# A two-layer hybrid diffusion trunk: weights loaded earlier at the start, PSUM operands in short VectorE chains, S5 states in fewer operations

## The chip, the cores and the metric

The kernel runs on one core of a Trainium2 chip. The metric is the time of one execution on the device in microseconds (us); the median of three runs stands for a kernel. One execution is also recorded by the profiler, and all rows below come from that one.

## What is computed

Two layers of one trunk, on a latent stream `x` of 512 tokens and a context of 256 tokens, both 1024 wide, in float32. The conditions `c` and `c_ctx` give six modulation vectors each (shift, scale and gate, twice). In each layer both streams go through four mixers side by side, are merged with gates, and pass a SwiGLU feed-forward part:

```python
mod_l = silu(c) @ w_ada[l] + b_ada[l]            # six vectors: sh1, sc1, g1, sh2, sc2, g2
h = rms_norm(x, norm1_g[l]) * (1 + sc1) + sh1    # the context the same way, with its own six
p = h @ w_in[l]                                  # columns for the four mixers and the gates
# S5: diagonal complex state space, forwards and backwards; gMLP; Mamba-2 SSD; latent attention
x = x + g1 * (merged @ w_out[l])
x = x + g2 * swiglu(rms_norm(x, norm2_g[l]) * (1 + sc2) + sh2)
```

`rms_norm` divides by the root of the mean square of a token's 1024 values. Latent attention norms its low-rank queries and keys once per token and then once per head; the SSD mixer norms its output, and gMLP has a layer norm. The context is not needed behind layer 1's mixers, so layer 1 carries it only as far as it is read.

## The kernel before, in words

Activations lie with channels on the 128 partitions and tokens along the free axis: eight tiles of 128 channels by 768 tokens, the first 256 the context (`CTXS`), the others the latent stream (`LAT`). Every large product is taken with each operand split into a high part in float32r and a low part that is the rest (`mm3`): three matmuls in place of one. Weights come in blocks of 1024 x 256 through two buffers (`weights`), ScalarE casts the high part, and GpSimd or VectorE subtracts the low part (`split`, L169 and L174).

The order on each engine is made by the framework's scheduler, which works through the program's instructions in program order with priorities, and holds an instruction back while its buffers are not free. The S5 mixer and the latent-attention pairs are generators that the program steps in turn, so that their small work lies between the projections.

What the change touches:

- **The start** (`run`, `ada_first`, `mix`). The latent stream is loaded, then `w_ada` for the first two vectors in three groups of columns (`ada_first`, L405), then the context and the first weights of `w_in`. The modulation is computed from the groups (`ada_chunk`), the latent stream normed (`norm_scale`) and modulated (`norm_mod`), then the context is transposed, normed and modulated. Only behind both stands `mix`, which takes the first two tiles of weights and projects them for the latent columns and then for the context's.
- **The norms** (`norm_scale`, `tok_rsqrt`, `rsqrt`). ScalarE squares eight tiles, VectorE adds them up in an SBUF tile (L174), a matmul with ones sums over channels, and `rsqrt` finds the inverse root per token: a bit estimate and two refinements, nine VectorE steps on 1 to 12 columns that each wait for the one before. `bcast_tok` puts the result on diagonals (L190), and a matmul spreads it. `mla_pair` uses `rsqrt` a second time, for six heads and two blocks of tokens.
- **The S5 mixer** (`s5_prep`, `s5_sixth`), in six parts a layer. `s5_prep` makes the operands of a sixth; four copies of 64x64 on VectorE (L479) stack real and imaginary halves. `s5_sixth` runs the scans and forms the states that enter each position, `sin`, in two tiles: forward and backward directions, real and imaginary halves, the backward ones written in reversed order, with three VectorE operations for each of four combinations.

Tiles from one pool carry its name: `sc`, `ty`, `f`, `g` and `h` are SBUF, `acc` (2 banks), `b1` (4) and `b5` (2) are PSUM and show as `acc` and `b`.

Of the kernel before, what the change touches and what calls it, by code (L numbers as in the profile page):

```python
# [12 lines left out]
I32 = mybir.dt.int32  # L13
AF = mybir.ActivationFunctionType
ALU = mybir.AluOpType
# [4 lines left out]
P = 128  # L20
D = 1024
KD = D // P
# [4 lines left out]
BR = 384  # L27
# [13 lines left out]
C_CQ = 2188  # L41
# [44 lines left out]
class Net:  # L86
# [116 lines left out]

    def rsqrt(s, y, x):
        t, u = s.ty(list(x.shape)), s.ty(list(x.shape))
        s.ts(y.bitcast(I32), x.bitcast(I32), -0.5, float(0x5F3759DF), ALU.mult, ALU.add)
        s.mul(t, y, y)
        s.mul(t, t, x)
        s.ts(u, t, 0.375, -1.25, ALU.mult, ALU.add)
        s.mul(u, u, t)  # L210
        s.stt(y, u, 1.875, y, ALU.add, ALU.mult)
        s.stt(t, y, -0.5, y, ALU.mult, ALU.mult)
        s.mul(t, t, x)
        s.stt(y, t, 1.5, y, ALU.add, ALU.mult)

# [53 lines left out]
    def tok_rsqrt(s, sq, nb, mul, eps):  # L269

        ps = s.b1()
        for b in range(nb):
            s.mm(ps[:, b * P:(b + 1) * P], sq[:, b * P:(b + 1) * P], s.ones)
        x, r = s.ty([P, nb]), s.ty([P, nb])
        s.ts(x, ps[:, 0:nb * P:P], mul, eps, ALU.mult, ALU.add)
        s.rsqrt(r, x)
        return r
# [118 lines left out]

    def ada_first(s, l):

        src = s.t["w_ada"][l].rearrange("(k p) f -> p k f", p=P)
        out = []  # L400
        for pool, tag, c, w, cuts in ((s.hp, "h", 0, 768, (0, 512, 768)), (s.hp, "h", 768, 768, (0, 256, 768)), (s.fp, "f", 1536, 512, (0, 512))):
            rows = []
            for k in range(KD):
                raw = pool.tile([P, w], F32, tag=tag, name=s.nm(tag))
                s.dma.dma_start(out=raw, in_=src[:, k, c:c + w])  # L405
                rows.append(raw)
            for a, b in zip(cuts, cuts[1:]):
                out.append(((c + a) // 256, b - a, [x[:, a:b] for x in rows]))
        return out

# [73 lines left out]
    def norm_scale(s, xs, off, n):  # L484

        sl = slice(off, off + n)
        a = s.sc()
        for k in range(KD):
            if k == 0:
                s.act(a[:, :n], xs[k][:, sl], AF.Square)  # L490
            else:
                q = s.sc()
                s.act(q[:, :n], xs[k][:, sl], AF.Square)
                s.add(a[:, :n], a[:, :n], q[:, :n])
        return s.bcast_tok(s.tok_rsqrt(a, n // P, 1.0 / D, 1e-6), n // P)
# [149 lines left out]
    def mla_pair(s, part, q, kd, off, t0, b0, xd, nk, nw, wh, wl, qk):  # L645

        eps = 1e-6
        w = 96 if part == "q" else 64
        hw = nw // 2
        x = s.st([P, nk, 256])  # L650
# [3 lines left out]
        sq, z = s.sc(), s.sc()  # L654
# [5 lines left out]
        r = s.tok_rsqrt(sq, 2, 1.0 / (nk * P), eps)  # L660
# [5 lines left out]
        for b in range(2):  # L666
            full = s.g()
            x = full[:, :576].rearrange("p (h d) -> p h d", d=96)
            z = s.st([P, 6, 96])
            for j in range(2):  # L670
                ps = s.b1()
# [13 lines left out]
        y, rs, rr = s.ty([P, 2, 6]), s.ty([P, 2, 6]), s.ty([P, 2, 6])  # L685
# [7 lines left out]
        s.ts(y, ms, 1.0 / 96, eps, ALU.mult, ALU.add)  # L693
        s.rsqrt(rs, y)
        s.mul(rr, rs, r.unsqueeze(2).to_broadcast([P, 2, 6]))
        gt, gc = q["rot"][part], q["gain"][:, 2 * (part == "kv") + (off == CTX):][:, :1]
        e = s.nc.gpsimd
        for b in range(2):
            x, full = tiles[b]
# [12 lines left out]
            y = full[:96].rearrange("p (h t) -> p h t", t=P)  # L712
            ps = [s.b1([P, 3, P]) for _ in range(2)]
# [368 lines left out]
    def s5_prep(s, l, i6):  # L1082

        gp, V = s.nc.gpsimd, s.nc.vector
        C, U = 96, 4
# [9 lines left out]
        for d in range(2):  # L1095
            o = 24 * l + 12 * d + 2 * i6
# [3 lines left out]
        x = [f_([P, U, C]) for _ in range(4)]  # L1100
# [13 lines left out]
        bbr, bbi, t1, t2 = (s.ty5([P, U, 16]) for _ in range(4))  # L1114
# [7 lines left out]
        for e in range(2):  # L1122
            s.vcopy(bbs[e][0:64], bbr[64 * e:64 * e + 64])
            s.vcopy(bbs[e][64:P], bbi[64 * e:64 * e + 64])

        pw = lambda k: G[:, k, :, 0:8].unsqueeze(3).to_broadcast([P, U, 8, 16])
        ch = lambda v: v.unsqueeze(2).to_broadcast([P, U, 8, 16])
        x = [f_([P, U, P]) for _ in range(4)]
# [37 lines left out]
    def s5_sixth(s, l, i6, ud, yd, segs):  # L1166
# [53 lines left out]
        yield  # L1220
        sin = [s.f([P, U, C]) for _ in range(2)]
        for e in range(2):
            gp.memset(sin[e][:, 0:2, 0:1], 0.0)
            gp.memset(sin[e][:, 2:4, 31:32], 0.0)
            r = slice(64 * e, 64 * e + 64)
            for w, (a, b, op) in zip((slice(0, 64), slice(64, P)), ((y[0], y[2], ALU.subtract), (y[1], y[3], ALU.add))):
                s.tt(sin[e][w, 0:2, 1:96], a[r, 0:2, 0:95], b[r, 0:2, 0:95], op)
                s.tt(sin[e][w, 2:4, 30::-1], a[r, 2:4, 0:31], b[r, 2:4, 0:31], op)
                s.tt(sin[e][w, 2:4, 95:31:-1], a[r, 2:4, 31:95], b[r, 2:4, 31:95], op)
        yield  # L1230
        ps = s.b5([C, 4, P])
        for i in range(2):
            for e in range(2):
                o = ps[:, 2 * i + e, :]
                s.mm(o, xf[:, 2 * i + e, :], tp[:, i, e, :], stop=False)
                s.mm(o, sin[e][:, i, :], ca[e][:, i, :], start=False, stop=False)
                s.mm(o, sin[e][:, 2 + i, :], ca[e][:, 2 + i, :], start=False)
        ys = s.f([C, 8, 4, 16])
# [41 lines left out]

    def mix(s, l, q, xs, xd, hh, hl, segs, rest, ws):

# [13 lines left out]
        def to_dram(d, segs_, f=None):  # L1296
            y = s.gs()

            def cb(ps, off, n, v):
                (f or s.act)(y[:, off:off + n], ps)  # L1300
                if off == segs_[-1][0]:
                    s.spill(d[:, off:], y[:, off:])
            return cb
# [11 lines left out]
        ws = ws or s.weights(w_in, C_CQ, BR)  # L1315
        pair = [(next(ws), to_dram(dq[c * P:(c + 1) * P], segs)) for c in range(2)]
        for sg in segs:
            for w, cb in pair:
                s.proj(w, hh, hl, [sg], cb)
        s.proj(next(ws), hh, hl, segs, to_dram(dq[2 * P:BR], segs))  # L1320
        next(load, None)
# [136 lines left out]

    def layer(s, l, q, f, xs, hh, hl, xd, extra, rest, late, then, ws=None):
        full = l < DEPTH - 1  # L1460
        segs = [LAT, CTXS] if full else [LAT]
        yd, gd = s.mix(l, q, xs, xd, hh, hl, segs, rest, ws)
        mh, ml = s.merge(l, yd, gd, segs)
# [71 lines left out]
    def run(s):  # L1535
# [3 lines left out]
        xr = s.load_x()  # L1539
        chunks = s.ada_first(0)  # L1540
        xr = s.load_ctx() + xr
        ws = s.weights(s.t["w_in"][0], C_CQ, BR)
        first = next(ws)
        q = turn({})
# [14 lines left out]
        def rest(a, lo, hi):  # L1559
            for i in range(lo, hi):  # L1560
                s.ada_chunk(a, i)
                yield
# [14 lines left out]
        next(norm)  # L1577
        next(xt)
        next(norm)
        s.params_more(0, q)  # L1580
        L8 = 21
        s.s5_scalars()
        ex = prepare()
# [9 lines left out]

        s.layer(0, q, a["f"], xs, hh, hl, xd, ex, rest(a, 8, L8), rest(a, L8, 24), then, chain([first], ws))
        xd = [s.dram(f"x1_{k}", [P, TOK]) for k in range(KD)]
# [34 lines left out]
```

## Time and profile before

| | before |
|---|---|
| median of three runs | 2789.63 us (2784.95 to 2795.59) |
| the profiled execution | 2790.0 us, span 2787.9 us |
| TensorE matmuls (PE) | 2626.4 us, 94% of the span |
| VectorE (DVE) | 1476.7 us, 53% |
| GpSimd (POOL) | 1211.5 us, 43% |
| ScalarE (ACT) | 940.7 us, 34% |
| mean granted TensorE clock | 0.978 |
| DMA | 397.32 MB, mean 143 GB/s |

A line of instructions reads: line of the program, engine, operation, output <- inputs by the program's names with their numbers left out, and shapes as partitions x elements. PE is TensorE's matmuls. A timeline row begins with the start and the length in us; xN means N instructions merged, and the bracket holds the idle time of the engine just before, with the instruction that ended it. Where several are merged, the length runs from the start of the first to the end of the last.

### The profile page before, as it was taken

What the parts mean: (1) busy time and instruction counts of PE and PEld (TensorE: products, weight loads), DVE (VectorE), ACT (ScalarE), POOL (GpSimd) and SP (SyncE); (2) the same over time, 40 slices, a digit from 0 to 9 for tenths busy, and PEclk for the clock granted to TensorE, in tenths of its full rate; (3) what the DMA queues carried; (4) which work ended last, traced back from release to release, by engine and by line L of the source; (5) the groups of instructions that cost most, each with busy time, mean ns of one, the idle gap of its engine ahead of it and who ended that gap; (6) DMA issues with size and microseconds to landing.
All of it is one profiled execution on the core that took longest, in us unless ns stands there. A gap on an engine that the chain in (4) does not pass through costs nothing. (4 is left out here: it accounts for less than half of the span.)

```text
span 2787.9 us, 39957 instructions
## 1 busy us (share of the span) xinstructions
PE 2626.4 (94%) x14964; PEld 2135.9 (77%) x14964; DVE 1476.7 (53%) x3088; ACT 940.7 (34%) x1805; POOL 1211.5 (43%) x901
## 2 busy tenths in 40 slices
PE   7998899999999998999999999999999999899999
PEld 4787777777888876888888877877766777678887
DVE  6667878647553768643321245676747446422111
ACT  4243344552222343222222234345552223322222
POOL 3254544324442836554433335443324536444443
PEclk8999999999999998999999999999999999999999
DMA  6655635445544645323322324566545546333332
GB/s 250 177 175 185 182 121 183 148 146 155 159 140 155 209 142 157 117 92 89 99 77 62 91 93 154 187 188 186 157 138 164 180 152 204 114 94 106 93 105 77
DMA packets 426040, 397.32 MB, mean 143 GB/s; under 512 B 53092, under 2 KB 372248, under 8 KB 425752
## 3 DMA queue, kind: packets, MB, share of 16 engines
q1 hardware_dynamic: 425848, 394.78, 45.8%
q8 instruction: 118, 1.93, 0.3%
q14 instruction: 74, 0.61, 0.1%
HBM read 305.66 MB, written 89.05 MB: 142 GB/s over the span
## 5 line engine op out<-in xcount | busy, mean ns | idle before, releaser
L174 POOL TENSOR_TENSOR wlo<-raw,whi 128x1024 fp32r<-128x1024 f32 (+2 forms) x314 | 629.2, 2005 | 1054.8 <-ACT whi L169 942.9
L193 PE MATMUL acc<-h,whi 128*128 128x512 f32 (+2 forms) x3424 | 1023.4, 369 | 20.0 <-DVE gs L186 7.6
L193 PE MATMUL acc<-h,wlo 128*128 128x512 f32 (+1 forms) x2024 | 747.8, 370 | 10.3 <-DVE wlo L174 5.5
L193 PEld LDWEIGHTS acc<-h,whi 128*128 128x128 f32 (+1 forms) x3424 | 613.4, 191 | 135.6 <-issue 15.7
L169 ACT CAST whi<-raw 128x1024 fp32r<-128x1024 f32 (+2 forms) x390 | 324.8, 834 | 775.3 <-PE b L193 300.8
L193 PEld LDWEIGHTS acc<-h,wlo 128*128 128x128 f32 x2024 | 385.2, 190 | 81.4 <-POOL wlo L174 8.5
L193 PE MATMUL acc<-g,whi 128*128 128x512 f32 (+1 forms) x840 | 270.2, 394 | 21.2 <-DVE g L174 8.1
L193 PE MATMUL acc<-f,whi 128*128 128x512 f32 (+1 forms) x600 | 230.4, 394 | 5.1 <-POOL f L174 5.1
L193 PE MATMUL b<-g,whi 128*128 128x256 f32 (+1 forms) x840 | 212.5, 331 | 3.3 <-ACT whi L169 3.3
L193 PE MATMUL b<-h,wlo 128*128 128x256 f32 (+1 forms) x624 | 203.6, 326 | 0.8 <-POOL wlo L174 0.8
L193 PE MATMUL b<-h,whi 128*128 128x256 f32 (+1 forms) x624 | 203.7, 326 | 0.0
L193 PEld LDWEIGHTS acc<-g,whi 128*128 128x128 f32 x840 | 153.2, 192 | 56.6 <-DVE g L174 11.7
L193 PE MATMUL b<-f,whi 128*128 128x256 f32 (+1 forms) x600 | 186.6, 321 | 1.5 <-ACT whi L169 1.5
L193 PE MATMUL b<-g,g 128*64 128x128 f32 (+5 forms) x915 | 177.8, 349 | 1.7 <-DVE g L190 1.1
L193 PEld LDWEIGHTS b<-g,whi 128*128 128x128 f32 x840 | 146.9, 191 | 28.1 <-ACT whi L169 6.5
L193 PE MATMUL acc<-g,wlo 128*128 128x512 f32 (+1 forms) x372 | 147.0, 395 | 4.3 <-DVE wlo L174 4.1
L186 DVE SCALAR_TENSOR_TENSOR sc<-sc,acc 128x512 f32<-128x512 f32 (+1 forms) x45 | 30.7, 681 | 218.9 <-ACT sc L171 218.9
L174 POOL TENSOR_TENSOR f<-f,f 128x384 f32<-128x384 f32 (+2 forms) x84 | 107.3, 1283 | 75.4 <-DVE f L174 36.5
L193 PEld LDWEIGHTS b<-g,g 128*128 128x128 f32 (+2 forms) x915 | 120.6, 180 | 22.7 <-issue 13.1
L174 POOL TENSOR_TENSOR g<-sc,g 128x256 fp32r<-128x256 f32 (+2 forms) x81 | 86.6, 1071 | 114.4 <-ACT g L169 88.3
L193 PEld LDWEIGHTS acc<-f,whi 128*128 128x128 f32 x600 | 113.0, 189 | 29.4 <-POOL f L174 6.6
L174 POOL TENSOR_TENSOR g<-g,sc 128x512 f32<-128x512 f32 (+1 forms) x82 | 102.6, 1261 | 68.5 <-DVE sc L186 35.7
(267 smaller groups left out, 3973.4 us busy)
## 6 DMA issues: line engine op xcount, KB each, us to landing
raw<-in_w_in_dram SPq DMA_DIRECT2D x50, 1024.0 KB
raw<-in_w_ffn_in_dram SPq DMA_DIRECT2D x88, 512.0 KB
raw<-in_w_ada_dram SPq DMA_DIRECT2D x40, 1024.0 KB
raw<-in_w_ffn_out_dram SPq DMA_DIRECT2D x36, 512.0 KB
gate<-gs SPq DMA_DIRECT2D x32, 384.0 KB
f<-s5w SPq DMA_DIRECT2D x48, 256.0 KB
raw<-in_w_branch_dram SPq DMA_DIRECT2D x32, 384.0 KB
gs<-gate SPq DMA_DIRECT2D x32, 384.0 KB
```

Source lines behind the costliest of these rows:

```text
L169: s.nc.scalar.copy(out=out, in_=x)
L174: (e or s.nc.vector).tensor_tensor(out=out, in0=a, in1=b, op=op)
L186: s.nc.vector.scalar_tensor_tensor(out=out, in0=a, scalar=sc, in1=b, op0=op0, op1=op1)
L193: s.nc.tensor.matmul(out=out, lhsT=l, rhs=r, start=start, stop=stop)
```

## The change

- `ada_first` takes a callback that it calls ahead of the third group of columns; `run` passes the loading and splitting of the first tile of weights, so this load of 1 MB (L525) is issued there and no longer behind the context.
- The context's transposes, norm and modulation, with the smaller parameters, go into a function `ctx` that `mix` calls behind the first tile's projection of the latent columns. `s5_scalars` moves behind the first two tiles.
- `rsqrt` computes the same two refinements in nine steps, ordered so that with `work` given each step has one operand in PSUM. `tok_rsqrt` passes two strips of the bank that it has, `mla_pair` a bank of its own. gMLP's five calls have no `work`. `norm_scale` adds up in a PSUM bank; the last addition writes SBUF.
- In `s5_prep` the four copies go to ScalarE. In `s5_sixth` VectorE writes `sin` for all four columns in forward order, four operations for twelve, and ScalarE writes the backward half reversed into a further tile `back`, in four copies.

```diff
-    def rsqrt(s, y, x):
-        t, u = s.ty(list(x.shape)), s.ty(list(x.shape))
-        s.ts(y.bitcast(I32), x.bitcast(I32), -0.5, float(0x5F3759DF), ALU.mult, ALU.add)
-        s.mul(t, y, y)
-        s.mul(t, t, x)
+    def rsqrt(s, y, x, work=None):
+
+        z, t = s.ty(list(x.shape)), s.ty(list(x.shape))
+        v, u = work or (y, s.ty(list(x.shape)))
+        s.ts(v.bitcast(I32), x.bitcast(I32), -0.5, float(0x5F3759DF), ALU.mult, ALU.add)
+        s.mul(z, x, v)
+        s.mul(t, z, v)
         s.ts(u, t, 0.375, -1.25, ALU.mult, ALU.add)
-        s.mul(u, u, t)
-        s.stt(y, u, 1.875, y, ALU.add, ALU.mult)
-        s.stt(t, y, -0.5, y, ALU.mult, ALU.mult)
-        s.mul(t, t, x)
-        s.stt(y, t, 1.5, y, ALU.add, ALU.mult)
+        s.mul(t, t, u)
+        s.stt(v, t, 1.875, v, ALU.add, ALU.mult)
+        s.mul(z, x, v)
+        s.stt(t, z, -0.5, v, ALU.mult, ALU.mult)
+        s.stt(y, t, 1.5, v, ALU.add, ALU.mult)
...
-        s.rsqrt(r, x)
+        s.rsqrt(r, x, [ps[:, c:c + nb] for c in (32, 40)])
...
-    def ada_first(s, l):
+    def ada_first(s, l, between):
...
             rows = []
+            if tag == "f":
+                done = between()
...
     def norm_scale(s, xs, off, n):
 
         sl = slice(off, off + n)
-        a = s.sc()
+        a, ps = s.sc(), s.b1()
         for k in range(KD):
             if k == 0:
-                s.act(a[:, :n], xs[k][:, sl], AF.Square)
+                s.act(ps[:, :n], xs[k][:, sl], AF.Square)
             else:
                 q = s.sc()
                 s.act(q[:, :n], xs[k][:, sl], AF.Square)
-                s.add(a[:, :n], a[:, :n], q[:, :n])
+                s.add((a if k == KD - 1 else ps)[:, :n], ps[:, :n], q[:, :n])
...
-        s.rsqrt(rs, y)
+        work = s.b1([P, 2, 2, 6])
+        s.rsqrt(rs, y, [work[:, j] for j in range(2)])
...
-            s.vcopy(bbs[e][0:64], bbr[64 * e:64 * e + 64])
-            s.vcopy(bbs[e][64:P], bbi[64 * e:64 * e + 64])
+            s.act(bbs[e][0:64], bbr[64 * e:64 * e + 64])
+            s.act(bbs[e][64:P], bbi[64 * e:64 * e + 64])
...
         sin = [s.f([P, U, C]) for _ in range(2)]
+        back = s.f([P, 2, 2, C])
         for e in range(2):
-            gp.memset(sin[e][:, 0:2, 0:1], 0.0)
-            gp.memset(sin[e][:, 2:4, 31:32], 0.0)
+            gp.memset(sin[e][:, :, 0:1], 0.0)
             r = slice(64 * e, 64 * e + 64)
             for w, (a, b, op) in zip((slice(0, 64), slice(64, P)), ((y[0], y[2], ALU.subtract), (y[1], y[3], ALU.add))):
-                s.tt(sin[e][w, 0:2, 1:96], a[r, 0:2, 0:95], b[r, 0:2, 0:95], op)
-                s.tt(sin[e][w, 2:4, 30::-1], a[r, 2:4, 0:31], b[r, 2:4, 0:31], op)
-                s.tt(sin[e][w, 2:4, 95:31:-1], a[r, 2:4, 31:95], b[r, 2:4, 31:95], op)
+                s.tt(sin[e][w, :, 1:96], a[r, :, 0:95], b[r, :, 0:95], op)
+
+            s.act(back[:, e, :, 31::-1], sin[e][:, 2:4, 0:32])
+            s.act(back[:, e, :, 95:31:-1], sin[e][:, 2:4, 32:96])
...
-                s.mm(o, sin[e][:, 2 + i, :], ca[e][:, 2 + i, :], start=False)
+                s.mm(o, back[:, e, i, :], ca[e][:, 2 + i, :], start=False)
...
-        pair = [(next(ws), to_dram(dq[c * P:(c + 1) * P], segs)) for c in range(2)]
-        for sg in segs:
+        pair = []
+        for c in range(2):
+            pair.append((next(ws), to_dram(dq[c * P:(c + 1) * P], segs)))
+            s.proj(pair[c][0], hh, hl, segs[:1], pair[c][1])
+            if c == 0 and ctx:
+                ctx()
+        for sg in segs[1:]:
             for w, cb in pair:
                 s.proj(w, hh, hl, [sg], cb)
+        if l == 0:
+            s.s5_scalars()
...
-        chunks = s.ada_first(0)
+        ws = s.weights(s.t["w_in"][0], C_CQ, BR)
+        chunks, first = s.ada_first(0, lambda: next(ws))
         xr = s.load_ctx() + xr
-        ws = s.weights(s.t["w_in"][0], C_CQ, BR)
-        first = next(ws)
...
-        next(xt)
-        next(norm)
-        s.params_more(0, q)
+
+        def ctx():
+            next(xt)
+            next(norm)
+            s.params_more(0, q)
```

The matmuls of the program are the same in kind and number. Three places show what moved.

First, GpSimd at the start. `wlo<-raw,whi` are the two splits of the first weights, `h<-sc,h` the low parts of the modulated latent stream, tile by tile. Before:

```order
L174 TENSOR_TENSOR h_449<-sc_457,h_441 128x512
L1004 MEMSET g_782 128x576
L1033 MEMSET g_834 128x48x4
L174 TENSOR_TENSOR h_451<-sc_465,h_443 128x512
...
L174 TENSOR_TENSOR h_455<-sc_481,h_447 128x512
L1057 MEMSET g_881 128x576
L174 TENSOR_TENSOR wlo_198<-raw_195,whi_197 128x1024
L174 TENSOR_TENSOR wlo_1082<-raw_195,whi_1081 128x1024
L174 TENSOR_TENSOR h_456<-sc_485,h_448 128x512
```

With the change:

```order
L174 TENSOR_TENSOR wlo_174<-raw_171,whi_173 128x1024
L1004 MEMSET f_937 128x48
L174 TENSOR_TENSOR wlo_731<-raw_171,whi_730 128x1024
L174 TENSOR_TENSOR h_450<-sc_458,h_442 128x512
L1009 MEMSET g_942 128x576
L1038 MEMSET g_994 128x48x4
L174 TENSOR_TENSOR h_452<-sc_466,h_444 128x512
```

The splits stood between the fifth and the sixth of GpSimd's subtractions and now stand ahead of the first.

Second, TensorE at the same place. `b<-k,f` transposes a block of the context, `acc<-h,whi` and `acc<-h,wlo` are the first projections of the latent columns. Before, the last of sixteen transposes and what follows:

```order
L197 MATMUL b_513<-k,f_193 128x128
L197 MATMUL b_517<-k,f_189 128x128
L197 MATMUL b_517<-k,f_193 128x128
L193 MATMUL acc_1086<-h_449,whi_197 128x512
L193 MATMUL acc_1086<-h_441,whi_197 128x512
```

With the change:

```order
L197 MATMUL b_571<-k,f_193 128x128
L193 MATMUL acc_537<-h_450,whi_173 128x512
L193 MATMUL acc_537<-h_442,whi_173 128x512
L193 MATMUL acc_537<-h_442,wlo_174 128x512
...
L193 MATMUL acc_735<-h_443,wlo_731 128x512
L197 MATMUL b_563<-k,f_197 128x128
```

Three of the context's transposes stand ahead of the first projections, the others between them.

Third, VectorE in the second norm of layer 0, context part: the last addition of the squares, the chain of `rsqrt` (`ty`, 128x2), and S5 products of layer 1's `s5_prep` (`h<-sx,sx`). Before:

```order
L174 TENSOR_TENSOR sc_10969<-sc_10969,sc_10989 128x256
L174 TENSOR_TENSOR h_11484<-h_11484,h_11485 128x512
L190 TENSOR_SCALAR ty_10995<-b_10992 128x2
...
L186 SCALAR_TENSOR_TENSOR ty_10998<-ty_10996 128x2
L174 TENSOR_TENSOR h_11633<-sx_11323,sx_11321 128x512
L174 TENSOR_TENSOR h_11635<-sx_11323,sx_11321 128x512
L174 TENSOR_TENSOR ty_10998<-ty_10998,ty_10995 128x2
L186 SCALAR_TENSOR_TENSOR ty_10996<-ty_10998,ty_10996 128x2
L190 TENSOR_SCALAR sc_11009<-k,ty_10996 128x128 x2
```

With the change:

```order
L174 TENSOR_TENSOR sc_10951<-b_10952,sc_10972 128x256
L174 TENSOR_TENSOR h_11467<-h_11467,h_11468 128x512
L190 TENSOR_SCALAR ty_10978<-b_10975 128x2
...
L174 TENSOR_TENSOR ty_10981<-ty_10978,b_10975 128x2
L174 TENSOR_TENSOR h_11616<-sx_11306,sx_11304 128x512
L174 TENSOR_TENSOR h_11618<-sx_11306,sx_11304 128x512
L186 SCALAR_TENSOR_TENSOR ty_10982<-ty_10981,b_10975 128x2
L186 SCALAR_TENSOR_TENSOR ty_10979<-ty_10982,b_10975 128x2
L190 TENSOR_SCALAR sc_10992<-k,ty_10979 128x128 x2
```

The neighbours are the same, two S5 products still stand inside the chain, and the chain's steps have a PSUM operand (`b`).

## Rows read from the trace of the kernel before

**Rows 1.** The page, part 1: busy time by engine, share of the span, instructions.
```profile
PE 2626.4 (94%) x14964; PEld 2135.9 (77%) x14964; DVE 1476.7 (53%) x3088; ACT 940.7 (34%) x1805; POOL 1211.5 (43%) x901
```
**Rows 2.** Waits of PE: waiter, what ended the wait; us in total, times, longest.
```profile
PE b L193 <- DVE sc L174: 14.2, 7, 4.0
...
PE b L193 <- DVE sc L190: 10.8, 3, 4.9
```
**Rows 3.** Timeline of PE at three places: start us, us, instruction, idle before.
```profile
247.59 1.49 PE L197 MATMUL b<-k,g 128*96 128x128 f32 x6 [9.92 <-DVE g L174]
...
1059.23 1.22 PE L193 MATMUL b<-ones,sc 128*128 128x128 f32 x4 [4.00 <-DVE sc L174]
...
1070.28 1.22 PE L193 MATMUL b<-sc,ones 128*128 128x256 f32 x2 [4.93 <-DVE sc L190]
```
**Rows 4.** Groups of DVE by shape: busy us, mean ns; idle before, releasers.
```profile
L479 DVE COPY ty<-ty 64x64 f32<-64x64 f32 x48 | 34.9, 727 | 0.7
L174 DVE TENSOR_TENSOR sc<-sc,sc 128x512 f32<-128x512 f32 x28 | 32.6, 1165 | 9.0 <-ACT sc L171 8.2
...
L174 DVE TENSOR_TENSOR sc<-sc,sc 128x256 f32<-128x256 f32 x26 | 28.9, 1112 | 2.3 <-ACT sc L171 0.5
...
L174 DVE TENSOR_TENSOR sc<-sc,acc 128x512 f32<-128x512 f32 x21 | 14.4, 687 | 70.4 <-PE acc L193 70.4
...
L174 DVE TENSOR_TENSOR sc<-sc,b 128x256 f32<-128x256 f32 x22 | 9.3, 421 | 45.1 <-PE b L193 45.0
```
**Rows 5.** Timeline of all engines, second norm of layer 0.
```profile
1064.71 1.58 POOL L174 TENSOR_TENSOR h<-h,h 64x512 f32<-64x512 f32 x1 [0.75 <-POOL h L174]
...
1065.10 3.51 DVE L174 TENSOR_TENSOR ty<-ty,ty 128x2 f32<-128x2 f32 x1
...
1066.27 2.33 POOL L174 TENSOR_TENSOR wlo<-raw,whi 128x1024 fp32r<-128x1024 f32 x1
```
**Rows 6.** Timeline of DVE, two steps of a chain in latent attention.
```profile
215.51 0.17 DVE L190 TENSOR_SCALAR ty<-ty 128x2 int32<-128x2 int32 x1
215.72 0.16 DVE L174 TENSOR_TENSOR ty<-ty 128x2 f32<-128x2 f32 x1
```
**Rows 7.** Timeline of PE, first projections: latent columns, then the context's.
```profile
44.60 2.07 PE L193 MATMUL acc<-h,whi 128*128 128x512 f32 x4 [1.35 <-ACT whi L169]
...
64.08 0.80 PE L193 MATMUL acc<-h,whi 128*128 128x256 f32 x2 [2.23 <-POOL h L174]
```
**Rows 8.** Timeline of the other engines from 30 to 54 us.
```profile
30.00 0.59 ACT L169 COPY gs<-acc 128x512 f32<-128x512 f32 x1 [0.43 <-PE acc L193]
...
33.37 1.27 POOL L174 TENSOR_TENSOR h<-sc,h 128x512 fp32r<-128x512 f32 x1 [0.85 <-ACT h L171]
...
38.49 0.17 DVE L186 SCALAR_TENSOR_TENSOR gs<-mod,prma 128x8 f32<-128x8 f32 x1
...
43.42 1.98 ACT L169 CAST whi<-raw 128x1024 fp32r<-128x1024 f32 x2
...
45.50 4.87 POOL L174 TENSOR_TENSOR wlo<-raw,whi 128x1024 fp32r<-128x1024 f32 x2
...
46.02 7.65 DVE L174 TENSOR_TENSOR sc<-sc,sc 128x256 f32<-128x256 f32 x6 [0.51 <-ACT sc L171]
```
**Rows 9.** Stretch from 25 to 30 us: busy us (count) by engine, clock, DMA, GB/s.
```profile
25.00:30.00 5.00, 5.00 (x31) 1.82 (x28) 3.55 (x9) 0.37 (x1) 0.00 (x0) 1.00 1.05 389
```
**Rows 10.** Timeline of DVE, copies of a sixth's preparation.
```profile
238.22 1.26 DVE L479 COPY ty<-ty 64x64 f32<-64x64 f32 x2
...
240.49 3.51 DVE L479 COPY ty<-ty 64x64 f32<-64x64 f32 x2
```
**Rows 11.** Two stretches: length, PE, PEld, DVE, ACT, POOL busy us, granted clock.
```profile
300.00:400.00 100.00, 86.10 (x506) 70.72 (x505) 77.68 (x160) 41.68 (x89) 48.20 (x44) 0.92 0.53 155
1000.00:1100.00 100.00, 81.29 (x484) 67.02 (x483) 82.44 (x133) 39.19 (x64) 55.70 (x41) 0.90 0.49 154
```
**Rows 12.** Timeline of DVE, the states of one sixth.
```profile
212.18 3.11 DVE L174 TENSOR_TENSOR f<-f,f 64x190 f32<-64x190 f32 x12
```

More of the change, by code (lines that the diff above doesn't have):

```diff
@@ L408, in ada_first @@
                 out.append(((c + a) // 256, b - a, [x[:, a:b] for x in rows]))
-        return out
+        return out, done
     def ada_chunk(s, a, i, w=256, raw=None):
@@ L1278, in s5_glu, with mix @@
             yield
-    def mix(s, l, q, xs, xd, hh, hl, segs, rest, ws):
+    def mix(s, l, q, xs, xd, hh, hl, segs, rest, ws, ctx):
         t = s.t
@@ L1457, in merge, with layer @@
         return mh, ml
-    def layer(s, l, q, f, xs, hh, hl, xd, extra, rest, late, then, ws=None):
+    def layer(s, l, q, f, xs, hh, hl, xd, extra, rest, late, then, ws=None, ctx=None):
         full = l < DEPTH - 1
         segs = [LAT, CTXS] if full else [LAT]
-        yd, gd = s.mix(l, q, xs, xd, hh, hl, segs, rest, ws)
+        yd, gd = s.mix(l, q, xs, xd, hh, hl, segs, rest, ws, ctx)
         mh, ml = s.merge(l, yd, gd, segs)
@@ L1577, in run @@
         next(norm)
-        next(xt)
-        next(norm)
-        s.params_more(0, q)
+        def ctx():
+            next(xt)
+            next(norm)
+            s.params_more(0, q)
         L8 = 21
-        s.s5_scalars()
         ex = prepare()
@@ L1592, in then @@
             next(nxt["norm"])
-        s.layer(0, q, a["f"], xs, hh, hl, xd, ex, rest(a, 8, L8), rest(a, L8, 24), then, chain([first], ws))
+        s.layer(0, q, a["f"], xs, hh, hl, xd, ex, rest(a, 8, L8), rest(a, L8, 24), then, chain([first], ws), ctx)
         xd = [s.dram(f"x1_{k}", [P, TOK]) for k in range(KD)]
```

## The prediction

> **What bounds the kernel now.** I read the page first: TensorE is busy for 2626.4 us, 94% of the span [rows 1], and the change takes no matmul away or adds one, so only TensorE's 161 us of idle time, and what its clock loses around them, can be won. Next I read who ends that idle time. A large share of the long waits end on a VectorE instruction, among them the two lines of the norms, 14.2 us for the sums and 10.8 us for the diagonals [rows 2]. The third view is the places: 9.92 us before the transposes of a latent-attention pair, and 4.00 and 4.93 us in the second norm of layer 0 [rows 3]. The reader is to see that TensorE is the bound, but that VectorE, at 53%, is late at particular places.
>
> The fourth view says why it is late. The same addition of 128x512 takes 1165 ns when both inputs lie in SBUF and 687 ns when one is a PSUM bank; at 128x256 it is 1112 against 421 ns, and a copy of 64x64, SBUF to SBUF, takes 727 ns, more than the PSUM addition with four times the elements [rows 4]. So the SBUF forms are not slow, they are held up. One place shows by whom: a multiplication of 128x2 takes 3.51 us and ends just as GpSimd ends the second of two long instructions that began at 1064.71 and 1066.27 [rows 5]. The same kind of step, left alone, takes 0.16 to 0.17 us and the next follows 0.21 us after it started [rows 6].
>
> The last view is the start. TensorE begins the first projection at 44.60 us and the context's columns at 64.08, after a wait on GpSimd [rows 7]. In between the two splits of the weights hold GpSimd for 4.87 us, and six additions of the context's norm take 7.65 us beside them, where 0.42 us each would be 2.5 [rows 4, 8].
>
> **The change, part by part.** The profiled execution took 2790.0 us, 2787.9 of it span; the median of the three runs is 2789.63, so the sum can be read against either.
>
> *Weights ahead, context behind the first tile.* No transfer is added. One megabyte moves ahead of the modulation's last quarter; at 389 GB/s [rows 9] that is 2.7 us, by which the quarter and the context come later. The casts (1.98 us) then stand behind the copy that ends at 30.6, in place of 43.42, and the splits fill GpSimd from about 31.6 to 36.5. Three of the six subtractions of 1.27 us follow; the other three wait for the second half of the scale, 38.49 plus 2.7 us, or 41.2, and with ScalarE's step and the clears between them they end near 47 [rows 8]. TensorE works through the latent columns as they come. The context's sums can follow ScalarE's last latent step at about 44: seven additions of 0.42 us, paced by squares of the same size, to 49, then the chain of 2.0 us, diagonals, broadcast and first scaling, so context matmuls at about 55 in place of 64.08. I take **-9 us**. The smaller end is -3: the norm starts no earlier than before and only sheds the stretch of 5.1 us, less part of the 2.7. The larger is -13, with nothing between sums and squares. The third tile's cast waits for the first tile's weights to be released, so it moves with them. The parameters and S5 scalars that are issued later are VectorE and DMA work beside projections; I cost that at nothing as long as projections cover it (rival one is the case without that cover).
>
> *Copies to ScalarE.* 48 copies, 34.9 us of VectorE [rows 4], become ScalarE work, on an engine at 34% [rows 1]. In front of the 9.92 us wait four of them take 1.26 and 3.51 us [rows 10]; these 4.8 us stand in VectorE's queue ahead of the scaling that TensorE waits for: **-5 us**, from -3 (the next two-input instruction meets GpSimd instead) to -9 (the chain beside them is freed as well). In the stretch from 300 to 400 us TensorE is idle for 13.9 us with VectorE at 78% [rows 11]; two sets of four copies lie there, 5.8 us at the mean. **-3 us**, from 0 to -6.
>
> *PSUM in the chains.* 39 of the 44 chains of nine steps and the 49 additions of seven norm parts get a PSUM operand. No operation is added, but a bank is held. In the second norm the context's chain of layer 0 holds the 3.51 us step [rows 5], and two of the additions' 4.00 us are the same effect: of 8.9 us there [rows 3] I take **-5**, from 0 (the wait is handed on) to -8. The other waits on the two norm lines come to 10.2 and 5.9 us [rows 2, 3]; most belong to additions that stay in SBUF or end on TensorE's own order, so a quarter: **-4**, from 0 to -8. What VectorE pays to write PSUM no row shows. The nearest rows read it, and there a PSUM operand costs nothing beyond the elements [rows 4], so I take the 0.21 us step as it is; the other end is a doubled step.
>
> [...]
>
> *States in four operations.* Twelve instructions took 3.11 us where nothing held them up [rows 12]. From the 687 and 421 ns [rows 4] an element costs 1.04 ns, so their 1520 elements cost 1.6 us and a start 0.13; four instructions come to 2.1 us. That is 1 us in each of 12 calls off VectorE, and fewer chances to meet GpSimd. Against it each call waits for four small ScalarE copies before the last matmuls. Both lie beside projections: **0**, from -3 to +12 (1 us at every call).
>
> *The clock and the order.* In the stretch from 1000 to 1100 us TensorE was granted 0.90 of its clock, and 0.92 from 300 to 400 [rows 11]. With half of that idle time gone and 0.90 turned into 0.95, 81.29 us of work shrink by 4.3. **-3 us** over the kernel, from 0 to -6. The scheduler wrote the order of both mixing stages anew, with the same matmuls; a new order can put a transpose before its input as well as after it. **+4 us**, from 0 to +10.
>
> Sum: -9 -5 -3 -5 -4 +0 -3 +4 = -25, so **2765 us**.
>
> **The rivals.**
> 1. *The start's gain is swallowed.* TensorE reaches the latent-attention stage 9 us sooner, but that stage waits for VectorE's S5 work and for its own weights. For: VectorE's 78% from 300 to 400 [rows 11]. Against: the scalars are released sooner too. 2790 - 16 = 2774 us. Chance 0.17.
> 2. *The hold-up is handed on,* so the change does not do what it says. Behind a chain stand the diagonals (SBUF to SBUF) and S5 products with two SBUF inputs; GpSimd's two instructions [rows 5] then hold one of those, and TensorE waits for the diagonals anyway. The -9 of the chains go and the -5 at the copies becomes -2: 2790 - 13 = 2777 us. Chance 0.13.
> 3. *Slow PSUM steps.* A doubled step costs 1.9 us a chain, on the path in seven norms: 2765 + 13 = 2778 us. Chance 0.08.
> 4. *Banks run short.* Four banks serve latent attention's matmuls and transposes. Now a chain of 2.0 us holds one from its matmul to its last step, two chains in each of 11 pairs. If TensorE waits for each of the 22, that is 44 us: 2790 - 25 + 44 = 2809 us, slower. It decides from the point where the remaining banks are not emptied before TensorE needs the next. Against: ScalarE, which empties most of them, is busy for 34% of the span [rows 1]. Chance 0.07.
> 5. *All of it comes:* the larger ends at the start, at the copies and in the norms together, 2745 us. Chance 0.05.
>
> **How the numbers follow.** The forecast has 0.50. A measurement of this kernel can tell 0.5% (14 us, or 2776) from no change. Faster takes nine tenths of the forecast, half of rival 1, under half of 2 and 3, and all of 5: 0.45 + 0.09 + 0.08 + 0.05, about 0.66 as I round down for the order that is new; slower than 2804 is most of rival 4 and a little besides, 0.07; 0.27 is left. The range takes in the forecast's own bounds and rivals 1 to 3, and leaves out 4 and the lower half of 5: 2738 to 2788 us.
>
> **What would show it.** Right: weights cast near 31 us, the context's first matmul near 55, the wait of 9.92 us under 5, norm additions at 128x512 near 0.69 us and at 128x256 near 0.42, no chain step above 0.3 us, VectorE's total down by 80 us or more. Wrong: chain steps of 0.3 us or more throughout (rival 3); diagonals or S5 products that swell where the chain no longer does (rival 2); transposes of the pairs that wait for a bank's release (rival 4); or a start that is 9 us ahead at 70 us and level at 300 (rival 1).

## The result

The changed kernel takes 2748.82 us (median of 4 runs, 2747.15 to 2749.48), the kernel before 2790.61 in the same comparison: a ratio of 0.985, 95% interval 0.983 to 0.987. It is faster by 1.5%, 42 us. The forecast was 2765 us, with a range from 2738 to 2788. Range and sign hold; most of the terms behind them do not.

The page of the changed kernel, part 1, and the two lines of the norms among the waits of TensorE, which answer [rows 1, 2]:

```profile
PE 2610.8 (95%) x14964; PEld 2132.2 (78%) x14964; DVE 1394.4 (51%) x2944; ACT 960.1 (35%) x1901; POOL 1219.8 (44%) x877
```
```profile
PE b L193 <- DVE sc L190: 11.4, 5, 3.1
...
PE b L193 <- DVE sc L174: 8.9, 7, 2.8
```

VectorE gave up 82.3 us. TensorE's busy time, with the same 14964 matmuls, fell by 15.6 us; the mean granted clock rose from 0.978 to 0.981, which by the estimate further below accounts for at most some 9 of them; the others are not explained. The idle rest of the span, 161.5 us before, is 135.6. So the 41.5 us between the two spans are some 26 of idle time and some 16 of matmuls that ran shorter.

Where they came is read at fixed points of TensorE's program: the starts of its 500th, 4000th, 9500th and 13500th matmul, which bound the start, layer 0's mixing, the stretch to the end of layer 0's feed-forward part, layer 1's mixing, and the end. The stretches, of the kernel before and then of the changed one (columns as in [rows 11]):

```profile
117.52:706.24 588.72, 547.21 (x3504) 441.45 (x3502) 416.02 (x962) 248.65 (x556) 247.77 (x214) 0.97 0.53 161
...
1679.48:2445.57 766.09, 718.19 (x4002) 556.15 (x4001) 450.08 (x944) 300.43 (x589) 328.53 (x246) 0.98 0.53 164
```
```profile
114.01:682.87 568.86, 540.22 (x3504) 440.86 (x3502) 389.88 (x890) 259.62 (x608) 257.44 (x203) 0.97 0.55 168
...
1648.15:2403.89 755.74, 716.05 (x4003) 558.27 (x4002) 424.67 (x896) 304.79 (x613) 328.96 (x234) 0.98 0.53 166
```

The start gained 3.5 us (117.5 to 114.0), layer 0's mixing 19.9, the middle 8.0, layer 1's mixing 10.4, the end nothing. What each part of the change did there can't be told from these two traces. The same division of every kernel that was run, one profiled execution each (the column of runs has the medians; "offset 250" is the same instructions in another order, below):

| kernel | runs | start | mixing 0 | middle | mixing 1 |
|---|---|---|---|---|---|
| before | 2790.6 | 117.5 | 588.7 | 973.2 | 766.1 |
| before, offset 250 | 2783.9 | 115.3 | 590.2 | 970.0 | 768.7 |
| copies alone | 2776.5 | 111.5 | 580.6 | 965.9 | 772.7 |
| states alone | 2783.1 | 117.8 | 586.1 | 974.6 | 765.8 |
| PSUM alone | 2807.2 | 112.7 | 591.3 | 969.9 | 787.9 |
| PSUM alone, offset 250 | 2785.0 | 115.6 | 592.2 | 964.7 | 767.7 |
| changed | 2748.8 | 114.0 | 568.9 | 965.3 | 755.7 |
| changed, offset 250 | 2745.8 | 114.8 | 572.9 | 969.3 | 748.6 |
| start undone | 2744.1 | 112.1 | 565.5 | 967.8 | 755.5 |
| copies undone | 2768.4 | 112.0 | 591.3 | 967.5 | 759.8 |
| PSUM undone | 2770.6 | 110.0 | 570.5 | 972.7 | 770.8 |
| sums alone undone | 2747.9 | 115.2 | 564.3 | 969.2 | 755.9 |
| states undone | 2775.8 | 114.0 | 565.5 | 968.0 | 787.9 |
| best | 2740.1 | 115.9 | 565.2 | 964.9 | 750.4 |

How finely can this be read? Where two kernels have the same instructions in a stage, in the same order on TensorE but for a few matmuls, their profiles can still lie 3 to 7 us apart: 568.9, 565.5 and 565.2 in layer 0's mixing (changed, start undone, best), 969.9 and 964.7 in the middle (PSUM alone at both offsets), 766.1 and 772.7 in layer 1's mixing, where no copy runs (before, copies alone). A difference of that size between two rows says little by itself.

The places of [rows 3] in the changed kernel, timeline of TensorE:

```profile
240.38 1.49 PE L197 MATMUL b<-k,g 128*96 128x128 f32 x6 [3.64 <-DVE g L174]
...
1030.13 1.22 PE L193 MATMUL b<-ones,sc 128*128 128x128 f32 x4 [2.36 <-DVE sc L174]
...
1039.41 1.22 PE L193 MATMUL b<-sc,ones 128*128 128x256 f32 x2 [3.07 <-DVE sc L190]
```

The wait of 9.92 us is 3.64, those of 4.00 and 4.93 are 2.36 and 3.07. The instructions did what the forecast said of them, but for the states, whose four operations were to take 2.1 us. Groups of VectorE by shape, and of ScalarE, which answer [rows 4, 12]:

```profile
L174 DVE TENSOR_TENSOR f<-f,f 64x380 f32<-64x380 f32 x48 | 34.2, 712 | 6.5 <-POOL f L174 3.9 <-POOL f L1229 1.8
...
L174 DVE TENSOR_TENSOR b<-b,sc 128x512 f32<-128x512 f32 x24 | 16.8, 698 | 4.2 <-ACT b L171 2.6 <-ACT sc L171 0.7
...
L190 DVE TENSOR_SCALAR b<-ty 128x2 int32<-128x2 int32 x14 | 2.3, 161 | 0.5
```
```profile
L169 ACT COPY ty<-ty 64x64 f32<-64x64 f32 x48 | 11.7, 243 | 28.9 <-DVE ty L174 28.5
```

A sum of 128x512 takes 698 ns for 1165, a chain's step into PSUM 161, a copy of 64x64 on ScalarE 243 for 727, and one of the four operations of the states 712. Whether such a gain reaches TensorE is another question, and the experiments are about that.

### The profile page after: what moved, and what is told of

Same layout as the page of the kernel before. It is cut to its first block, busy times and chain, and to the rows that moved or that the text cites. A ratio compares the mean times of both kernels' runs of the same rounds, so it can differ in the third digit from the quotient of the medians.

```text
span 2746.4 us, 39879 instructions
## 1 busy us (share of the span) xinstructions
PE 2610.8 (95%) x14964; PEld 2132.2 (78%) x14964; DVE 1394.4 (51%) x2944; ACT 960.1 (35%) x1901; POOL 1219.8 (44%) x877
```

## The experiments

Theories: the **forecast's sum** (start 9, copies 8, PSUM 9 us, states nothing); **VectorE's load** (the gain goes with the VectorE time taken off, wherever it is); **the order** (the scheduler wrote the order anew, and that is what moved the time).

### One part undone

From the changed kernel, each line of `+` in place of that of `-`; with the PSUM part undone the steps of `rsqrt` and the call in `tok_rsqrt` are as before too:

```diff
# start undone
-        chunks, first = s.ada_first(0, lambda: next(ws))
+        chunks = s.ada_first(0)
...
+        first = next(ws)
...
# copies undone
-            s.act(bbs[e][0:64], bbr[64 * e:64 * e + 64])
+            s.vcopy(bbs[e][0:64], bbr[64 * e:64 * e + 64])
...
# PSUM undone (and the sums as further below)
-        work = s.b1([P, 2, 2, 6])
-        s.rsqrt(rs, y, [work[:, j] for j in range(2)])
+        s.rsqrt(rs, y)
...
# states undone
-                s.tt(sin[e][w, :, 1:96], a[r, :, 0:95], b[r, :, 0:95], op)
+                s.tt(sin[e][w, 0:2, 1:96], a[r, 0:2, 0:95], b[r, 0:2, 0:95], op)
...
```

> The changed kernel with only the start, the order of the first pair and the place of the S5 scalars as before. Forecast's sum: the start is worth 9 us, so 2758. Trace of the change: the lead at the 500th matmul (117 against 114 us) is 3.5 us, so 2752 if it is only that. Rival, VectorE's load: the start takes no VectorE work away, so 2749 to 2752. Rival, the order: any value between 2740 and 2775, with differences in places that this edit does not touch.

> The changed kernel with the 48 copies of 64x64 on VectorE again. Forecast's sum: 8 us, so 2757. Rival, VectorE's load (the 41 us gained went with 82 us of VectorE time taken off, one half per us): 35 us come back, so 2749 + 17 = 2766. Rival, the order: 2740 to 2775.

> The changed kernel with the sums of squares and all chains of the inverse root in SBUF, written as before. Forecast's sum: 9 us, so 2758, with sums at 128x512 near 1.17 us again. Rival, VectorE's load (18 us left for this part): 2749 + 9 = 2758 as well, but then the gain is spread over the mixing stages. Rival, the hold-up is only handed on: 2749 to 2751. Rival, slow PSUM steps: faster, near 2740.

> The changed kernel with the states of a sixth in twelve VectorE operations again and no copies on ScalarE for them. Forecast's sum: 0, so 2749 (from 2737 to 2752). Rival, VectorE's load: 29 us come back, so 2749 + 14 = 2763. Rival, the order: 2740 to 2775.

Measured against before: start undone 0.983 (0.981 to 0.985), copies 0.992 (0.990 to 0.994), PSUM 0.993 (0.991 to 0.995), states 0.996 (0.994 to 0.997). The start is worth nothing: without it the median is 4.7 us lower. The other three, undone singly, give back 19.6, 21.8 and 26.9 us, 68 together, where the whole change brought 42. They do not add up, and the table says where they act: the copies in layer 0's mixing (22 us, and 4 in layer 1), the states in layer 1's alone (32), the PSUM part in the middle (7) and in layer 1 (15). The states are used by six sixths in each layer, so VectorE's load would have shown in both.

Only one of the four is a part undone and nothing else. With the start undone TensorE's matmuls stand in the change's order but for a few (both traces compared by names and shapes). With the copies undone hundreds of them move in layer 0's mixing, with the PSUM part or the states undone hundreds in both layers' mixing, so each of these numbers is the part and an order together.

### One part alone

> The kernel before with only the 48 copies moved to ScalarE. Forecast's sum: 8 us, so 2780. VectorE's load, parts that add up: the 20 us that undoing this part cost, scaled by 46/69 (the gain of the three parts over the sum of what undoing them cost), so 2775, won in layer 0's mixing. Parts that need each other: 2784 to 2790. The order: anything from 2765 to 2795.

> The kernel before with only the sums of squares and the chains in PSUM. Forecast's sum: 9 us, so 2779. Parts that add up: 22 us scaled by 46/69, so 2774, with 5 us in layer 0's second norm. Parts that need each other: 2784 to 2790. The order: 2765 to 2795.

> The kernel before with only the states in four operations. Forecast's sum: 0, so 2788. Parts that add up: 27 us scaled by 46/69, so 2770, won in layer 1's mixing alone. The order: 2765 to 2795, in either layer.

From the kernel before, with the same edits turned round: copies alone 0.995 (0.994 to 0.997), states alone 0.997 (0.996 to 0.998), PSUM alone **1.005 (1.003 to 1.007), slower by 15 us**, outside every range that was set down for it. Load can't explain the last: the page of that kernel has VectorE at 1431.5 us, 45 below before. Its stretch in layer 1's mixing:

```profile
1673.84:2461.78 787.94, 731.62 (x4003) 566.80 (x4001) 434.80 (x944) 300.38 (x589) 330.25 (x246) 0.96 0.51 159
```

VectorE has 15 us less to do than before in the same part of the program, and TensorE takes 22 us longer, at a lower clock (0.96 for 0.98): 13 of them are matmuls that ran longer, 8 are idle time. Waits of TensorE in that stretch, before and then here:

```profile
PE b L193 <- DVE f L174: 6.1, 3, 4.7
```
```profile
PE b L193 <- DVE f L174: 13.3, 7, 4.8
```

The kernel with the states undone took 787.9 us there as well. It too has the PSUM part beside the states in twelve operations, and its matmuls in that stage stand in the order of this kernel but for a handful of 4000: the same order came out of both edits, and took the same time.

### The order alone

The S5 generator runs at a raised priority. Another offset moves the same instructions:

```diff
-        five = at(state_space(), 300)
+        five = at(state_space(), 250)
```

> The changed kernel with the same instructions in another order: the S5 generator's priority offset 250 in place of 300, which reorders TensorE's work in layer 0's mixing (some 2000 of 13513 matmul instructions) and a little in layer 1's. VectorE's load decides: within 5 us of 2749, as no work is added. The order decides: layer 0's mixing comes out 10 us or more apart, in either direction.

> The kernel with only the PSUM part (2807 us), with the S5 generator's offset 250 in place of 300: the same instructions, some 1400 of TensorE's 13513 in another place in layer 1's mixing and 1200 in layer 0's. From the 9500th to the 13500th matmul it took 788 us, the kernel before 766 and the change 756. If its order is what cost it: 775 or less there, so 2793 or less in all. If VectorE's or GpSimd's load decides: 788 within 5 again, 2802 to 2812 in all.

> The kernel before with the offset 250 in place of 300: the same instructions, 1400 of TensorE's in another place in layer 0's mixing and 950 in layer 1's. Layer 0's mixing (500th to 4000th matmul) took 589 us before and with every kernel that has the copies on VectorE (586 to 591), 565 to 581 with the copies on ScalarE. If VectorE's load decides: 584 to 594 there again. If the order decides: outside of that.

The slow layer 1 of the PSUM part was its order: 787.9 us became 767.7 with not an instruction changed, and the kernel went from 2807 to 2785. That leaves open how much of the 32 us with the states undone are the twelve operations, since they were not run in another order with the rest of the change. Stretch of the PSUM part at the new offset, with VectorE as busy as in the slow one:

```profile
1672.59:2440.29 767.70, 720.21 (x4001) 560.08 (x4001) 430.86 (x946) 302.42 (x590) 331.44 (x247) 0.98 0.53 165
```

The changed kernel is less sensitive (2745.8, with layer 0 4 us longer and layer 1 7 us shorter), the one before moved by 8 in the median and hardly in the mixing stages. There VectorE's load, or rather its place, decides: layer 0's mixing took 586 to 592 us in all six kernels with the copies on VectorE, in six different orders, and 564 to 581 in all eight with the copies on ScalarE.

### Why the copies

Copies of the kernel before from 100 to 720 us, one group:

```profile
L479 DVE COPY ty<-ty 64x64 f32<-64x64 f32 x28 | 23.1, 825 | 0.3
```

Seven sets of four; the other 20 copies lie in layer 0's feed-forward part, which takes as long with them as without (967.5 and 965.3 us for the middle). In the kernel with the copies undone, one of the places, VectorE and then TensorE:

```profile
234.90 0.16 DVE L174 TENSOR_TENSOR ty<-ty,b 128x12 f32<-128x12 f32 x1
...
235.11 1.27 DVE L483 COPY ty<-ty 64x64 f32<-64x64 f32 x2
236.41 0.17 DVE L190 TENSOR_SCALAR b<-ty 128x12 f32<-128x12 f32 x1
236.61 2.00 DVE L483 COPY ty<-ty 64x64 f32<-64x64 f32 x2
238.62 2.78 DVE L174 TENSOR_TENSOR f<-ty,f 128x512 f32<-128x512 f32 x1
241.33 0.15 DVE L174 TENSOR_TENSOR ty<-ty,b 128x12 f32<-128x12 f32 x1
```
```profile
244.29 1.49 PE L197 MATMUL b<-k,g 128*96 128x128 f32 x6 [9.35 <-DVE g L174]
...
318.12 1.22 PE L193 MATMUL acc<-h,whi 128*128 128x512 f32 x2 [6.57 <-DVE gs L186]
...
389.37 1.19 PE L193 MATMUL acc<-h,whi 128*128 128x512 f32 x2 [6.44 <-DVE gs L186]
```

Same two later places in the changed kernel:

```profile
312.77 1.22 PE L193 MATMUL acc<-h,whi 128*128 128x512 f32 x2 [3.08 <-DVE gs L186]
```
```profile
379.50 0.70 PE L193 MATMUL acc<-h,whi 128*128 128x512 f32 x2 [1.90 <-DVE gs L186]
```

The chain has every step in PSUM and each is short, but its steps stand between the copies and a product with SBUF operands: from the step at 234.90 to the one at 241.33 there are 6.4 us, of which steps are 0.3. Three waits of 22.4 us are 8.6 in the changed kernel. They lie where the copies come.

Not all of that is gained. At the first place the two scalings behind the chain take 1.43 us with the copies undone and 4.59 in the changed kernel, where a sum of 128x512 and a split of 128x1024 on GpSimd lie beside them (238.36 to 242.43 us); the first line is the kernel with the copies undone, the second the changed one:

```profile
243.39 1.43 DVE L174 TENSOR_TENSOR g<-g,ty 128x576 f32<-128x576 f32 x2
```
```profile
238.46 4.59 DVE L174 TENSOR_TENSOR g<-g,ty 128x576 f32<-128x576 f32 x2
```

What is left is read from the starts of every hundredth matmul in both traces. The changed kernel's lead grows by 2.7 us over the hundred matmuls at the second set of copies, 3.2 at the third, 4.3 at the fourth, and 3.4 and 3.6 right behind the fifth and sixth; around the first nothing settles. These are 17 of the 22 us in the stage.

### The sums alone, at an order kept

```diff
-        a, ps = s.sc(), s.b1()
+        a = s.sc()
...
-                s.add((a if k == KD - 1 else ps)[:, :n], ps[:, :n], q[:, :n])
+                s.add(a[:, :n], a[:, :n], q[:, :n])
```

> The changed kernel with only the sums of squares (norm_scale) in SBUF again; TensorE's order is the change's but for some 40 instructions, so this is load alone. Seven norms have 49 additions. If the hold-up by GpSimd costs what the forecast took: sums at 128x512 near 1.17 us again, a longer wait for them in layer 0's second norm (2.36 us in the change, 4.00 before), 2 to 8 us in all, so 2751 to 2757. If only the order counts: 2749 within 3.

2747.9 us, 0.984 (0.982 to 0.985): no difference from the change (0.985). Group and wait of that run:

```profile
L174 DVE TENSOR_TENSOR sc<-sc,sc 128x512 f32<-128x512 f32 x28 | 32.3, 1155 | 9.2 <-ACT sc L171 8.4
```
```profile
PE b L193 <- DVE sc L174: 10.2, 6, 3.7
```

The hold-up is back in full, VectorE is 18 us busier, and TensorE waits 1.3 us longer for sums. What the PSUM part is worth is in the chains, or in the order that comes with them: TensorE's order, which this edit leaves as it is, was another one in the kernel with the whole part undone.

### A faster version

```diff
-        five = at(state_space(), 300)
+        five = at(state_space(), 300 if l == 0 else 250)
```

with the start as before.

> The start as before, all else of the change, and the S5 generator's offset 250 in layer 1 alone. Layer 0 in the order of the kernel with the start undone (565 us from the 500th to the 4000th matmul), layer 1 in the order of the changed kernel with offset 250 (749 us from the 9500th to the 13500th, where the change took 756). If an order keeps its time in another kernel: 112 + 566 + 968 + 749 + 338 us, with what lies around it 2737. If the 7 us in layer 1 were chance: 2744.

2740.13 us (2736.94 to 2740.70), 0.981 (0.979 to 0.983). The median lies midway between the two that were expected, 2737 and 2744, and the start took 115.9 us where 112 was expected. Layer 1's mixing took 750.4 us, close to the 748.6 that the same order had taken in another kernel: there an order kept its time, and the order of the change took 755.5 to 755.9 in three kernels (changed, start undone, sums alone undone). The kernel is 8.7 us faster than the change, and no run of the one reaches the other's. How much of this is the order is seen in the stage alone: the runs of the kernel with only the start undone (2735.3 to 2745.5 us) take in all of these.

## Why the prediction was right, and where it was not

The time lay in the range because terms that were too large and terms that were too small went opposite ways, and that is luck. It is the time of rival 5, which had a chance of 0.05 (its larger ends add up to 2747, not to 2745), and not for its reasons: neither the start nor the norms gave their larger ends.

- **Start, -9 forecast: nothing that can be told from zero.** Two steps failed. The step "the splits fill GpSimd from about 31.6 to 36.5. Three of the six subtractions of 1.27 us follow" moved GpSimd's work and asked only when it would be done, not what runs beside it. And "The context's sums can follow ScalarE's last latent step at about 44" left out the context's own transposes. Timelines of the changed kernel, ScalarE, GpSimd, VectorE and TensorE:

```profile
30.89 1.99 ACT L169 CAST whi<-raw 128x1024 fp32r<-128x1024 f32 x2 [1.83 <-DMA raw<-in_w_in_dram]
...
43.89 2.22 ACT L171 ACTIVATE h<-g,mod,gs 128x512 fp32r<-128x512 f32 x3
```
```profile
32.01 2.35 POOL L174 TENSOR_TENSOR wlo<-raw,whi 128x1024 fp32r<-128x1024 f32 x1 [30.85 <-DMA f<-in_w_ada_dram]
...
34.40 2.58 POOL L174 TENSOR_TENSOR wlo<-raw,whi 128x1024 fp32r<-128x1024 f32 x1
```
```profile
32.19 7.19 DVE L190 TENSOR_SCALAR sc<-g,gs,mod 128x512 f32<-128x512 f32 x3 [0.42 <-DVE gs L186]
...
49.86 0.42 DVE L483 COPY g<-b 128x256 f32<-128x256 f32 x1 [1.08 <-PE b L197]
...
54.08 0.42 DVE L174 TENSOR_TENSOR sc<-b,sc 128x256 f32<-128x256 f32 x1
```
```profile
49.44 0.60 PE L197 MATMUL b<-k,f 128*128 128x128 f32 x4
...
50.56 0.60 PE L197 MATMUL b<-k,f 128*128 128x128 f32 x4
...
60.90 0.80 PE L193 MATMUL acc<-h,whi 128*128 128x256 f32 x2 [2.28 <-POOL h L174]
```

The weights are cast at 30.89, as forecast. But the splits now lie beside VectorE's three scalings of the latent stream, which take 7.19 us and took 3.15 before:

```profile
32.48 3.15 DVE L190 TENSOR_SCALAR sc<-g,gs,mod 128x512 f32<-128x512 f32 x3
```

The hold-up was carried from the context's additions (six took 7.65 us before [rows 8], five take 2.50 at 51.44 us in the changed kernel) to the latent's scalings, and ScalarE's last latent step ends at 46.1, 2 us late. From there the sums do not run on. The last eight of the context's sixteen transposes (`b<-k,f`) stand between projections in TensorE's order, at 49.44 and 50.56, and VectorE waits for them. The last transposes start at 42 to 43 us in the eight kernels with the old start and at 49 to 52 in the six with this one. So the last of the context's additions starts at 54.08 in place of a forecast end at 49, and the context's first matmul is at 60.90, not 55. The 3.2 us left of it are within what the start varies anyway: 110 to 115 us in the six profiles with this start, 111 to 118 in the eight with the old one.

- **Copies, -5 and -3 forecast: 15 us alone, 20 if undone.** Right mechanism, mis-sized terms. Against the kernel with the copies undone, the set in front of the 9.92 us wait gave 2.7 us and not 5, as the hold-up was handed on to the scalings (4.59 us for 1.43), the lower end of that term. The two sets from 300 to 400 us gave 7.5 and not 3: the step "two sets of four copies lie there, 5.8 us at the mean" took little more than half of the time of these copies. And the fifth and sixth sets, 7.0 us, are not in the sum (the seventh set's copies took 0.2 us each). Of the 15 us of the copies alone its profile has 8 in layer 0's mixing, against 20 in the whole change (580.6 us against 564 to 573 beside another part); 6 lie in the start, where no such copy runs. Why they are worth less alone is not explained.

- **PSUM in the chains, -5 and -4.** In layer 0's second norm 8.9 us of waits became 5.4, so -3.5 of the -5. Rival 2 took the rest. The other waits on the two lines went from 16.1 to 14.9 us, -1.2 of the -4. VectorE and GpSimd there, changed kernel, to be read beside [rows 5]:

```profile
1033.22 2.62 DVE L174 TENSOR_TENSOR h<-sx,sx 128x512 f32<-128x512 f32 x2
1035.77 0.34 DVE L186 SCALAR_TENSOR_TENSOR ty<-ty,b 128x2 f32<-128x2 f32 x2
1036.14 3.22 DVE L190 TENSOR_SCALAR sc<-k,ty 128x128 f32<-128x128 f32 x2
```
```profile
1035.26 1.71 POOL L174 TENSOR_TENSOR h<-h,h 64x512 f32<-64x512 f32 x1
1036.93 2.34 POOL L174 TENSOR_TENSOR wlo<-raw,whi 128x1024 fp32r<-128x1024 f32 x1
```

The chain's steps are short beside GpSimd's work (0.34 us for two, beside its 1.71), and the diagonals, SBUF to SBUF, take the 3.22 us in their place, ending within 0.1 us of the second GpSimd instruction. Before they took 1.37:

```profile
1068.85 1.37 DVE L190 TENSOR_SCALAR sc<-k,ty 128x128 f32<-128x128 f32 x2
```

Both lines of the norms together went from 25.0 to 20.3 us. Rival 3 is out: the groups of steps that read or write PSUM have means of 155 to 174 ns, and with SBUF sources, left alone, such steps took 160 to 170 [rows 6]. Rival 4's slower sign did come for this part alone, not by its mechanism: the added waits shown above end on VectorE, on tiles in SBUF, and another order takes the 20 us away with the same banks.

- **States, 0 from -3 to +12: 9 us gained alone, 27 lost if undone.** What failed is the idea that such a part has one price. Layer 1's mixing takes 788 us with the PSUM part and twelve operations, but 768 in another order, and 749 to 760 with four; without the PSUM part it is 766 to 773 with twelve, and 766 and 771 with four. So the 27 us are not shown to be the states' own, and whether "both lie beside projections" held was not tested at an order kept. What VectorE gave up was mis-sized too: four operations at 712 ns are 2.8 us and not 2.1, and yet the three groups that they replace took 63.2 us in all and they take 34.2, so 29 us went and not 12: the old ones took 5.3 us a call at the mean and not the 3.11 of the place that was read. Before:

```profile
L174 DVE TENSOR_TENSOR f<-f,f 64x190 f32<-64x190 f32 x48 | 25.8, 538 | 4.2 <-POOL f L174 3.2
...
L174 DVE TENSOR_TENSOR f<-f,f 64x128 f32<-64x128 f32 x48 | 20.2, 421 | 0.0
...
L174 DVE TENSOR_TENSOR f<-f,f 64x62 f32<-64x62 f32 x48 | 17.2, 358 | 0.0
```


- **Clock, -3 from 0 to -6: at most about -9, an estimate.** TensorE's pace went with the granted clock where both can be read: in the first projection of the kernel before, three matmuls of 128x512 (two of `acc<-h,whi`, one of `acc<-h,wlo`) start every 1.28 us from 48.51 to 52.35, at a clock of 0.50 from 48 to 53 us, and every 0.68 to 0.70 us from 55.77 to 60.56, at 1.00 from 55 to 61. Mean granted clocks of 0.978 and 0.981 leave 2.2% of the one span (2787.9 us) and 1.9% of the other (2746.4) not granted: 61 and 52 us. If TensorE is busy throughout, these 9 us less are worth 9. The two clocks are of one execution each; over its executions the kernel before had 0.971 to 0.980, the changed one 0.979 to 0.981.

- **Order, +4 from 0 to +10: the largest mis-size.** One reordering without any other change is worth 20 us in a single stage. The sign was forecast as a loss, and it can be either. In layer 1 the whole change gained 10 us, and the offset of 250 gains 5 to 7 more. Whether the four operations and the PSUM chains gain there by their time or by the order they lead to was tried no further than this, and stays open.

## What to carry to other kernels

When a scheduler writes the order, a part of a change has no price of its own: undo it, do it alone, and reorder it without any other change, and read each by stage before putting a number to it. An engine that is half idle can still set the time through a few short instructions that stand in its queue ahead of what the bound engine waits for, as VectorE did here at 51 to 53% of the span: three waits came to 22.4 us with its copies of 64x64 and to 8.6 without them. Count all the places of the kind, not only those at which a long wait shows. A hold-up between two engines can go to the next instruction that can be held, as it did in three places here (the scalings at the start took 7.19 us for 3.15, those of latent attention 4.59 for 1.43, the diagonals 3.22 for 1.37): look at what stands behind the one that is freed, and at what the other engine's moved work will lie beside. And work that is to start earlier needs all of its inputs earlier: look for the one that stays where it was in another engine's order.

## What the runs showed that was not expected

- The same program in another order took 788 and 768 us in one stage, with VectorE's and GpSimd's busy time the same within 4 us.
- An order kept its time in another kernel: 748.6 and 750.4 us in one stage, and 787.9 in two others that came to the same order by different edits. Not always: before and copies alone share one there, and took 766.1 and 772.7.
- Taking 45 us of work off an engine made the kernel 15 us slower, by the order that came with it.
- Sums of squares that took 1155 or 698 ns each gave the same time of the kernel within 1 us; TensorE's waits for them differ by 1.3 us.
